# A fp32 hybrid SSD block on one core: sums of the second merge branch taken inside the group norms, SiLU by three tiles, and first loads and splits of each stage issued sooner

## Chip, core and metric

The kernel runs on one core of a Trainium2 chip. The metric is the device time of one execution in microseconds (us). Every number below comes from the timed runs of the kernel, or from one profiled execution of it.

## What is computed

One block on `x` of 1024 rows by 1024 columns, all in float32: a norm, an input projection to 8 fields, a Mamba-2 scan (SSD) with a group norm, a short gated convolution, two gated branch projections and an output projection, then a SwiGLU with 2816 hidden columns and a last norm.

```python
u = h @ w_in                                   # h = rmsnorm(x, norm_mix_w)
z, xbc, dt_raw, s_b, s_c, s_x, g_a, g_b = jnp.split(u, IN_SPLITS, axis=-1)
xbc = silu(causal_depthwise_conv(xbc, ssd_conv_w) + ssd_conv_b)
y = ssd_chunked_scan(xs32, dt, a, bm32, cm32) + d_skip * xs32
y = y * silu(z)
yg = y.reshape(bsz, seqlen, SSD_GROUPS, SSD_INNER // SSD_GROUPS)          # 4 groups of 512
yg = yg * lax.rsqrt(jnp.mean(yg * yg, axis=-1, keepdims=True) + EPS)
branch_a = (yg * ssd_norm_w) @ w_ssd_proj
branch_b = (s_b * causal_depthwise_conv(s_c * s_x, sconv_w)) @ w_sconv_proj
h = x + (sigmoid(g_a) * branch_a + sigmoid(g_b) * branch_b) @ w_o
h = h + (silu(n @ w_gate) * (n @ w_up)) @ w_down                          # n = rmsnorm(h, norm_ffn_w)
return rmsnorm(h, final_norm_w)
```

## The kernel before

Every large product is one level of Winograd-Strassen: seven products (numbers n, in the order 1, 2, 6, 5, 7, 3, 4) of block sums such as `T1` to `T4` of the right operand and `S1` to `S4` of the left. Each fp32 operand is split into a high and a low part (names that end in h and l: `wh`/`wl` of a weight, `qh`/`ql` and `gh`/`gl` of a merge chunk, `th`/`tl` of rows), and a product is three matmuls, high by high, low by high, high by low. ACT (ScalarE) makes the high parts, DVE (VectorE) the low ones; a matmul on TensorE (PE) that needs a low part waits for DVE.

The stages follow each other, and the order of the work is written out by hand, so each engine executes its list in that order. All tiles of 4 KB per partition come from one pool of 47 pages; a load into a page waits until its last user is done. SP issues nearly all loads and stores, in one list.

1. Start, 0 to about 74 us: rows of `x` are normed (`rows_sq`, `rows_scale`), transposed on PE (tiles `pt`), split, and the first pairs of weights are multiplied. The second half of the rows (`second_half`) follows between these.
2. Slots of the input projection, to about 605 us.
3. Direct tiles, to about 994 us: 22 weight slabs `ws` (6 for `z`, 16 for the gates `ga`, `gb`), a plain product each (tile `pr`, matmuls at L81 to L83). Between them runs the SSD scan (loads `bc`, `x`, `ab`, `eb`; matmuls `pxt`, `poff`, `pdg`), and after each group and half of the rows its norm: `z` is loaded, POOL multiplies (L508), ACT squares, DVE reduces, the factor goes to DRAM and back as a broadcast tile (`rs_d`, `rbc`), DVE scales the rows (L538) and they are stored to `y_g`. `y_sums` then loads two groups back (`br<-y_g`), makes the sums `T1` to `T4` (L720 to L724) and stores them to `yt_d`.
4. Merge, to about 1290 us: chunks of three products (`gv` for branch b, `gy` for branch a, `go` for `w_o`); a chunk is 24 matmuls of 512 columns for a pair of k-tiles. `Stream.step` loads four chunks ahead and splits two ahead; `ms.ahead(loads, splits)` does the first of these while the last direct tiles run.
5. FFN units to about 1745 us, whose first rows (`h1_rows`, `fill`, `put`) are normed, transposed and split while the last chunks of `go` run, then the down product (`ds`) and the last norm.

Of the kernel before, what the change touches and what calls it, by code (L numbers as in the profile page):

```python
# [13 lines left out]
P = 128  # L14
# [4 lines left out]
G = 4  # L19
# [20 lines left out]
def hybrid_block(ctx: ExitStack, tc: tile.TileContext, x, nmw, w_in, cw, cb, dtb, alog, dsk, snw,  # L40
# [194 lines left out]
    nc.sync.dma_start(ra, cw[0].rearrange("k (i p) -> (k i) p", p=P))  # L235
    rb = cp.tile([80, P], F32, name="rb")
    nc.sync.dma_start(rb[0:8, :], nmw.rearrange("o (i p) -> (o i) p", p=P))
    nc.sync.dma_start(rb[8:16, :], nfw.rearrange("o (i p) -> (o i) p", p=P))
    nc.sync.dma_start(rb[16:40, :], cb.rearrange("o (i p) -> (o i) p", p=P))
    nc.sync.dma_start(rb[40:56, :], snw.rearrange("o (i p) -> (o i) p", p=P))  # L240
    nc.sync.dma_start(rb[56:80, :], scw[0].rearrange("k (i p) -> (k i) p", p=P))
# [5 lines left out]
    nc.sync.dma_start(d2, dsk.rearrange("o (i j) -> (o i) j", j=2))  # L247

    dtbc = cp.tile([H, 1], F32, name="dtbc")
    nc.sync.dma_start(dtbc, dtb.rearrange("o h -> h o"))  # L250
    al = cp.tile([P, 1], F32, name="al")
    for q in range(4):
        nc.sync.dma_start(al[32 * q:32 * q + 32, :], alog.rearrange("o h -> h o"))
# [94 lines left out]
    halves, norms = {}, []  # L348
# [147 lines left out]
    def norm(g, hf, y0, y1):  # L496
# [204 lines left out]
    def yk(l, k):  # L701

        return (k // 4) * 8 + 4 * l + k % 4
# [5 lines left out]
    def y_sums(q):  # L709

        store = None
        for r in range(4):
            r1, r2 = page("br", HB), page("br", HB)
            for t, g in ((r1, 2 * q), (r2, 2 * q + 1)):
                nc.sync.dma_start(t.rearrange("p a l -> p (a l)"), y_d[4 * g + r])
            if store is not None:
                store()
            yield
            t = page("bt", HB)
            V.tensor_add(t[:, 0, :], r1[:, 0, :], r1[:, 1, :])  # L720
            V.tensor_add(t[:, 1, :], t[:, 0, :], r2[:, 1, :])
            yield
            V.tensor_add(r1[:, 1, :], r1[:, 1, :], r2[:, 1, :])
            V.tensor_add(r2[:, 0, :], r2[:, 0, :], t[:, 1, :])  # L724
            yield

            def store(r=r, t=t, r1=r1, r2=r2):
                for f, o in (("T1", t[:, 0, :]), ("T2", t[:, 1, :]), ("T3", r1[:, 1, :]), ("T4", r2[:, 0, :])):
                    nc.sync.dma_start(yt_d[f][(4 * q + r) * P:(4 * q + r) * P + P, :], o)
        store()  # L730
        yield

    def all_weight_sums():
        yield from weight_sums("S", sc_d, [(wsc, a, wsc, 512 + a, a, 256) for a in (0, 256)])
        yield from weight_sums("S", ss_d, [(wssd, 1024 * q + a, wssd, 1024 * q + 512 + a, 512 * q + a, 256)
                                           for q in range(2) for a in (0, 256)])
# [231 lines left out]

    def z_raw(i):
        hold = []  # L970

        def f(ps, hf):
            if hf == 0:
                hold.append(page("gt"))
# [199 lines left out]
    def ffn_phase():  # L1174
# [182 lines left out]
        while ms.at < len(ms.chunks):  # L1357
# [4 lines left out]
            if c.n in (7, 4):  # L1362
                for _ in range(3):
                    next(rows, None)
# [96 lines left out]
        for i, (_, pe, ev) in enumerate(rest):  # L1461
            load_to(14 + i)
            while later and next(later[0], 0) == 0:
                later.pop(0)
            pe()
# [3 lines left out]
            if i >= len(rest) - 4:  # L1469
                ds.ahead(i - len(rest) + 5, i - len(rest) + 2)  # L1470
# [43 lines left out]
    for p in first:  # L1514
        p.x.load()
# [194 lines left out]
```

## Time and profile before

| | us |
|---|---|
| median of 3 timed runs | 1966.7 (1964.54 to 1967.37) |
| profiled execution, its own time | 1965.9 |
| span of the profiled execution | 1964.1 |
| outside the span | 1.8 |
| PE busy | 1903.3 of the span |
| DVE, ACT, POOL busy | 1294.5, 984.2, 176.4 |

A row of the timeline or of a group gives the start, the busy time, the engine, the line, the operation and the tiles (written tile, arrow, read tiles). A bracket at the end gives the idle time of that engine just before and what ended it. In a table of windows `PEclk` is the mean granted clock of TensorE, as a share of full speed (1.00 is 2.4 GHz, 0.50 is 1.2 GHz).

### The profile page before, as it was taken

How to read it: one execution, taken by the hardware profiler on the slowest of the kernel's cores; microseconds unless marked ns; L12 is line 12 of the kernel's file. 1: busy time of each engine (PE TensorE's matmuls, PEld its weight loads, DVE VectorE, ACT ScalarE, POOL GpSimd, SP SyncE). 2: the span in 40 equal slices, each digit the busy share in tenths (PEclk: the TensorE clock that was granted, in tenths of full speed). 3: DMA queues.
4: the chain of work that ended last, by engine and by line, in shares of the span. 5: the costliest groups of instructions: out<-in, count | busy, mean ns of one | idle time of the engine just before them, and what ended most of it. 6: DMA issues, size and time to landing. Idle time of an engine off the chain costs nothing.

```text
span 1964.1 us, 24428 instructions
## 1 busy us (share of the span) xinstructions
PE 1903.3 (97%) x8917; PEld 1560.3 (79%) x8917; DVE 1294.5 (66%) x1674; ACT 984.2 (50%) x1547; POOL 176.4 (9%) x156
## 2 busy tenths in 40 slices
PE   5999999999998999998999999989999999999998
PEld 4678888888886887887878888878888888878886
DVE  6757877777774779787868547867444444456465
ACT  5444444444446997866556454455333333335433
POOL 0001111111100011110200000101121112100000
PEclk9999999999999999998999999989999999999999
DMA  5087998899959567776889766834888888868552
GB/s 176 22 218 202 220 239 211 240 240 236 266 155 265 180 204 226 234 254 210 289 332 388 260 224 208 205 124 103 231 192 193 215 198 201 208 241 303 193 185 116
DMA packets 350833, 422.49 MB, mean 215 GB/s; under 512 B 19752, under 2 KB 226424, under 8 KB 350712
## 3 DMA queue, kind: packets, MB, share of 16 engines
q1 hardware_dynamic: 304248, 353.80, 54.7%
q0 software_dynamic: 43296, 55.58, 17.7%
q10 hardware_dynamic: 3168, 11.54, 1.5%
q8 instruction: 70, 1.15, 0.2%
q14 instruction: 51, 0.42, 0.1%
HBM read 328.95 MB, written 145.24 MB: 241 GB/s over the span
## 4 chain that ended last, share of the span: by engine, by line
PE 55%; DVE 3%; DMA 2%; ACT 2%; issue 1%; SPq 0%; ACTq 0%; DVEq 0%
PE gb L664 5%; PE gb L665 5%; PE gb L663 5%; PE fb L665 4%; PE fb L664 4%; PE fb L663 4%; PE gd L665 4%; PE gd L664 4%; PE gd L663 4%; PE fd L663 3%; PE fd L664 3%; PE fd L665 3%; PE pr L81 2%; PE pr L83 2%; PE pr L82 2%; PE pdg L483 1%
## 5 line engine op out<-in xcount | busy, mean ns | idle before, releaser
L77 DVE TENSOR_TENSOR wl<-ws,wh 128x1024 fp32r<-128x1024 f32 x77 | 94.0, 1222 | 123.2 <-ACT wh L76 123.2
L664 PE MATMUL gb<-ql,gh 128*128 128x512 f32 x432 | 169.6, 393 | 3.7 <-DVE ql L77 3.7
L663 PE MATMUL gb<-qh,gh 128*128 128x512 f32 x432 | 169.6, 393 | 3.1 <-ACT qh L76 3.1
L665 PE MATMUL gb<-qh,gl 128*128 128x512 f32 x432 | 168.9, 391 | 0.0
L83 PE MATMUL pr<-th,wl 128*128 128x512 f32 x352 | 139.0, 395 | 7.6 <-DVE wl L996 7.6
L81 PE MATMUL pr<-th,wh 128*128 128x512 f32 x352 | 145.5, 413 | 0.0
L663 PE MATMUL fb<-th,wh 128*128 128x512 f32 x352 | 138.5, 393 | 2.6 <-ACT th L76 2.0
L665 PE MATMUL fb<-th,wl 128*128 128x512 f32 x352 | 138.0, 392 | 0.8 <-DVE wl L77 0.8
L664 PE MATMUL fb<-tl,wh 128*128 128x512 f32 x352 | 138.2, 393 | 0.5 <-DVE tl L77 0.5
L82 PE MATMUL pr<-tl,wh 128*128 128x512 f32 x352 | 138.2, 393 | 0.0
L663 PE MATMUL gd<-qh,gh 128*128 128x512 f32 x324 | 126.0, 389 | 0.0
L664 PE MATMUL gd<-ql,gh 128*128 128x512 f32 x324 | 126.0, 389 | 0.0
L665 PE MATMUL gd<-qh,gl 128*128 128x512 f32 x324 | 126.0, 389 | 0.0
L76 ACT ACTIVATE qh<-cb 128x1024 fp32r<-128x1024 f32 x98 | 100.0, 1020 | 40.7 <-PE gb L664 17.2
L77 DVE TENSOR_TENSOR ql<-cb,qh 128x1024 fp32r<-128x1024 f32 x98 | 115.9, 1182 | 3.2 <-ACT qh L76 3.0
L665 PE MATMUL fd<-th,wl 128*128 128x512 f32 x264 | 102.7, 389 | 0.0
L663 PE MATMUL fd<-th,wh 128*128 128x512 f32 x264 | 102.7, 389 | 0.0
L664 PE MATMUL fd<-tl,wh 128*128 128x512 f32 x264 | 102.7, 389 | 0.0
L74 DVE SCALAR_TENSOR_TENSOR gl<-ca,gh 128x1024 fp32r<-128x1024 f32 (+1 forms) x60 | 70.6, 1177 | 43.4 <-ACT gh L73 43.4
L664 PEld LDWEIGHTS gb<-ql,gh 128*128 128x128 f32 x432 | 81.8, 189 | 21.2 <-DVE ql L77 4.3
L663 PEld LDWEIGHTS gb<-qh,gh 128*128 128x128 f32 x432 | 81.8, 189 | 20.8 <-ACT qh L76 3.8
L665 PEld LDWEIGHTS gb<-qh,gl 128*128 128x128 f32 x432 | 81.8, 189 | 17.0
(309 smaller groups left out, 4725.0 us busy)
## 6 DMA issues: line engine op xcount, KB each, us to landing
ws<-in_w_in_dram SPq DMA_DIRECT2D x80, 512.0 KB, 7.7
ws<-in_w_gate_dram SPq DMA_DIRECT2D x77, 256.0 KB, 3.8
ws<-in_w_up_dram SPq DMA_DIRECT2D x77, 256.0 KB, 4.1
ca<-u_d SPq DMA_DIRECT2D x35, 512.0 KB, 6.2
ab<-ac_d SPq DMA_DIRECT2D x32, 512.0 KB, 6.0
xbc_d<-cv SPq DMA_DIRECT2D x24, 512.0 KB, 3.2
ws<-ws POOLq DMA_DIRECT2D x22, 512.0 KB, 6.3
wd_d<-in_w_down_dram SPq DMA_DIRECT2D x20, 512.0 KB, 11.7
```

What stands on the lines that cost most here:

```text
L74: nc.vector.scalar_tensor_tensor(lo, src, -1.0, hi.bitcast(F32), op0=ALU.mult, op1=ALU.subtract)
L76: nc.scalar.activation(hi, src, AF.Copy)
L77: nc.vector.tensor_sub(lo, src, hi.bitcast(F32))
L81: nc.tensor.matmul(o, lh, rh, start=first, stop=False)
L82: nc.tensor.matmul(o, lh, rl, start=False, stop=False)
L83: nc.tensor.matmul(o, ll, rh, start=False, stop=last)
L483: nc.tensor.matmul(pdg[64 * i:64 * i + 64, r * P:(r + 1) * P], xx[:, 0, 2 * r + i, :], ab[:, 2 * r + i, :], start=True, stop=True)
L663: nc.tensor.matmul(o, lh, rh, start=first, stop=False, skip_group_check=True)
L664: nc.tensor.matmul(o, lh, rl, start=False, stop=False, skip_group_check=True)
L665: nc.tensor.matmul(o, ll, rh, start=False, stop=last, skip_group_check=True)
```

## The change

In the order of the program:

- Start. The small loads `ra` and `rb` are issued on ACT's queue, and `d2`, `dtbc`, `al` after the first weight slabs. One row tile of each half is scaled by POOL instead of ACT. On PE the first half's 32 transposes come first, with the first weight pairs and the first half of the step-size product right behind them; the second half's transposes follow after the first product of all three pairs.
- `pump_scan()` is called at `left == 8` instead of 4: the first loads of the scan come ahead of the store of a `z` tile and of the first direct slab on SP.
- The six direct `z` tiles are evicted with `Copy`, and SiLU is applied to three tiles at a time, in place, before their stores.
- `y_sums` is gone. The norm keeps the pages of the first half of a group (`kept`), and after the second half it forms the four sums with DVE adds of 128x1024 and stores them. With that the k-halves of the branch are inside a group (`yk`, the regrouped sums of `wssd`), and rows of the second half that only fed the sums are no longer stored.
- `ms.ahead` is called before a direct tile instead of after it, and `ds.ahead` before the matmuls of an FFN step.
- The steps of the first FFN rows are given to the last four chunks of `go` as 2, 4, 6 and 2 instead of 3 each.

```diff
@@ start
-    nc.sync.dma_start(ra, cw[0].rearrange("k (i p) -> (k i) p", p=P))
+    nc.scalar.dma_start(ra, cw[0].rearrange("k (i p) -> (k i) p", p=P))
...
-    r0 = rows_scale(*a0, act=(2, 3))
+    r0 = rows_scale(*a0, act=(2,), pool=(3,))
...
+    for k in range(4):
+        turn_rows(r0, k)
+    turned_out(raw0, 0)
+    turned_out(raw0, 1)
+    p0.hi("A1")
+    turned_out(raw0, 2)
+    turned_out(raw0, 3)
+    p0.lo("A1")
+    for k in range(4, 8):
+        turn_rows(r0, k)
+    every(put("B11", raw0[0]))
+    p0.pe(1)
+    wdt_split()
+    steps_pe(0, 0)
...
+    r1 = rows_scale(*a1, act=(2,), pool=(3,))
...
@@ norm of a group
-            nc.sync.dma_start(y_d[4 * g + r][:, o], z)
+            if hf == 0 or r > 1:
+                nc.sync.dma_start(y_d[4 * g + r][:, o], z)
             if r % 2:
                 yield
-        if g % 2 and hf:
-            aux.append(y_sums(g // 2))
+        if hf == 0:
+            kept[g] = ys
+            return
+
+        b11, b21 = kept.pop(g)
+        b12, b22 = ys
+        t1, t2 = page("s1", HB), page("s2", HB)
+        for t, a, b, f in ((t1, b11, b12, "T1"), (t2, t1, b22, "T2"), (b12, b12, b22, "T3"), (b21, b21, t2, "T4")):
+            V.tensor_add(t, a, b)
+            nc.sync.dma_start(yt_d[f][256 * g:256 * g + 256, :].rearrange("(k p) f -> p k f", p=P), t)
+            yield
...
@@ z tiles
-            nc.scalar.activation(hold[0][:, hf * 512:hf * 512 + 512], ps, AF.Silu)
-            if hf:
-                nc.scalar.dma_start(z_d[i], hold.pop())
+            nc.scalar.activation(z_held[-1][1][:, hf * 512:hf * 512 + 512], ps, AF.Copy)
+            if hf and len(z_held) == 3:
+                for k, t in z_held:
+                    nc.scalar.activation(t, t, AF.Silu)
+                    nc.scalar.dma_start(z_d[k], t)
+                z_held.clear()
...
@@ FFN
-            if c.n in (7, 4):
-                for _ in range(3):
-                    next(rows, None)
+            for _ in range({(7, 0): 2, (7, 2): 4, (4, 0): 6, (4, 2): 2}.get((c.n, c.k), 0)):
+                next(rows, None)
...
+            if i >= len(rest) - 4:
+                ds.ahead(i - len(rest) + 5, i - len(rest) + 2)
             pe()
             ev()
             if i + 2 < len(rest):
                 rest[i + 2][0]()
-            if i >= len(rest) - 4:
-                ds.ahead(i - len(rest) + 5, i - len(rest) + 2)
...
@@ end of the slots, direct tiles
-        if left == 4:
+        if left == 8:
             pump_scan()
...
     for i in range(len(direct)):
+        ms.ahead(i - len(direct) + 4, i - len(direct) + 2)
         direct_tile(i)
-        ms.ahead(i - len(direct) + 4, i - len(direct) + 2)
```

First place, SP's list around 590 us, at the end of the slots. Before (`z_d` is the store of a `z` tile, `ws` a slab of a direct tile; the others are loads of the scan):

```order
L597 DMA z_d_151<-u_4272 128x1024
L597 DMA z_d_152<-u_4333 128x1024
L165 DMA ws_4417<-in_w_in_dram 128x8x128
L359 DMA bc_4454<-xbc_d_137 128x256
...
L363 DMA x_562_4459<-xbc_d_123 128x512
L363 DMA x_562_4459<-xbc_d_124 128x512
L373 DMA ab_4462<-ac_d 128x1024
L373 DMA ab_4464<-ac_d 128x1024
L381 DMA eb_4466<-e_d 64x4x128 x2
L165 DMA ws_4499<-in_w_in_dram 128x8x128
```

The same place of the change:

```order
L609 DMA z_d_145<-u_4272 128x1024
L361 DMA bc_4376<-xbc_d_131 128x256
...
L365 DMA x_552_4381<-xbc_d_117 128x512
L365 DMA x_552_4381<-xbc_d_118 128x512
L375 DMA ab_4384<-ac_d 128x1024
L375 DMA ab_4386<-ac_d 128x1024
L383 DMA eb_4388<-e_d 64x4x128 x2
L609 DMA z_d_146<-u_4333 128x1024
L165 DMA ws_4432<-in_w_in_dram 128x8x128
L165 DMA ws_4499<-in_w_in_dram 128x8x128
```

The ten loads of the scan moved ahead of the second store of a `z` tile and of the first direct slab, which now is eleven rows further down.

Second place, DVE's list where the direct tiles end and the merge begins (about 994 us). L538 (L540 in the change) scales rows of the last group's norm with `rbc`; `gl` and `ql` are the low parts of a merge chunk, the first pair those of chunk 0. Before:

```order
L538 SCALAR_TENSOR_TENSOR y_7657<-y_7657,cols,rbc_8318 128x512 x2
L74 SCALAR_TENSOR_TENSOR gl_8365<-ca_8184,gh_8364 128x1024
L77 TENSOR_TENSOR ql_8369<-cb_8186,qh_8368 128x1024
L538 SCALAR_TENSOR_TENSOR y_7658<-y_7658,cols,rbc_8318 128x512 x2
L74 SCALAR_TENSOR_TENSOR gl_8386<-ca_8289,gh_8385 128x1024
L77 TENSOR_TENSOR ql_8390<-cb_8291,qh_8389 128x1024
```

The same place of the change (L553 are the adds that make the four sums):

```order
L74 SCALAR_TENSOR_TENSOR gl_8278<-ca_8032,gh_8277 128x1024
L77 TENSOR_TENSOR ql_8282<-cb_8034,qh_8281 128x1024
L540 SCALAR_TENSOR_TENSOR y_7657<-y_7657,cols,rbc_8309 128x512 x2
L540 SCALAR_TENSOR_TENSOR y_7658<-y_7658,cols,rbc_8309 128x512 x2
L553 TENSOR_TENSOR s_1254_8352<-y_7196,y_7657 128x1024
L553 TENSOR_TENSOR s_1255_8353<-s_1254_8352,y_7658 128x1024
L553 TENSOR_TENSOR y_7657<-y_7657,y_7658 128x1024
L553 TENSOR_TENSOR y_7197<-y_7197,s_1255_8353 128x1024
L74 SCALAR_TENSOR_TENSOR gl_8372<-ca_8169,gh_8371 128x1024
L77 TENSOR_TENSOR ql_8376<-cb_8171,qh_8375 128x1024
```

The pair of chunk 0 moved ahead of the rows that wait for `rbc`; the pair of chunk 1 now stands behind all four of these and four adds of 128x1024.

## Rows read from the trace of the kernel before

**Rows 1.** Top of the page of the whole run: the span, and busy time of each engine with its share of the span and its instructions.

```profile
span 1964.1 us, 24428 instructions
PE 1903.3 (97%) x8917; PEld 1560.3 (79%) x8917; DVE 1294.5 (66%) x1674; ACT 984.2 (50%) x1547; POOL 176.4 (9%) x156
```

**Rows 2.** Who kept PE waiting over the whole run: engine, tile and line that waited, what it waited for, us in total, times, longest us.

```profile
PE pc L1521 <- DMA ra<-in_ssd_conv_w_dram: 9.6, 1, 9.6
PE pr L83 <- DVE wl L996: 7.6, 2, 6.8
PE pxt L420 <- DMA bc<-xbc_d: 4.0, 1, 4.0
PE gb L664 <- DVE ql L77: 3.7, 2, 2.8
PE pt L148 <- DVE hn L137: 3.3, 2, 3.0
PE poff L469 <- ACT st L476: 3.2, 1, 3.2
PE gb L663 <- ACT qh L76: 3.1, 1, 3.1
PE fb L663 <- ACT th L76: 2.0, 1, 2.0
```

**Rows 3.** Windows around these waits: start and end, length, busy time of PE, PEld, DVE, ACT, POOL with the number of instructions, granted clock of PE, busy share of the DMA engines, GB/s.

```profile
13.00:28.00 15.00, 9.98 (x45) 7.89 (x45) 11.27 (x21) 10.46 (x16) 0.00 (x0) 1.00 1.07 342
28.00:36.00 8.00, 5.46 (x16) 3.57 (x16) 6.25 (x10) 6.82 (x10) 0.00 (x0) 0.57 0.13 44
604.00:609.00 5.00, 1.04 (x5) 0.54 (x3) 0.00 (x0) 0.94 (x1) 0.70 (x1) 1.00 1.11 295
904.00:916.00 12.00, 5.20 (x33) 3.85 (x33) 9.48 (x15) 6.38 (x17) 0.00 (x0) 0.88 0.98 345
916.00:924.00 8.00, 8.00 (x29) 7.01 (x28) 7.09 (x14) 3.89 (x13) 0.00 (x0) 0.55 0.79 239
1288.00:1297.00 9.00, 5.59 (x19) 3.84 (x19) 5.46 (x12) 5.61 (x7) 0.00 (x0) 0.81 0.00 0
1312.00:1325.00 13.00, 10.49 (x35) 7.89 (x34) 9.83 (x17) 7.21 (x13) 0.00 (x0) 0.74 0.30 123
```

**Rows 4.** Timeline of DVE at the start (row scaling) and, with POOL's only elementwise work in the trace, around 760 us: start, us, engine, line, operation, tiles, count.

```profile
12.36 1.42 DVE L137 TENSOR_SCALAR xn<-x,nr 128x1024 f32<-128x1024 f32 x2
...
758.68 5.46 POOL L508 TENSOR_TENSOR y<-y,z 128x1024 f32<-128x1024 f32 x2 [41.40 <-PE pst L83]
759.00 2.89 DVE L444 TENSOR_TENSOR xw<-xx,xw 128x512 fp32r<-128x512 f32 x1
764.61 0.68 DVE L470 TENSOR_TENSOR xx<-poff,eb 128x512 f32<-128x512 f32 x1
```

**Rows 5.** Timeline of SP, ACT and PE where the scan and the direct tiles begin, with one row of what SP waited for between 590 and 625 us.

```profile
587.85 4.03 SPq L597 DMA_DIRECT2D z_d<-u  x2
591.92 0.65 SPq L165 DMA_DIRECT2D ws<-in_w_in_dram  x1
592.67 9.15 SPq L359 DMA_DIRECT2D bc<-xbc_d  x4
601.93 1.16 SPq L363 DMA_DIRECT2D x<-xbc_d  x2
...
SPq L359 <- PE pd L664: 5.4, 1, 5.4
...
608.06 1.06 ACT L993 ACTIVATE wh<-ws 128x1024 fp32r<-128x1024 f32 x1 [6.50 <-DMA ws<-in_w_in_dram]
616.46 0.40 PE L81 MATMUL pr<-th,wh 128*128 128x512 f32 x1
```

**Rows 6.** Timeline of DVE where `y_sums` runs ahead of the low part of a direct slab, and of PE, which waits for that part.

```profile
903.71 0.69 DVE L720 TENSOR_TENSOR bt<-br 128x512 f32<-128x512 f32 x1 [5.72 <-DMA br<-y_g]
...
909.18 1.22 DVE L442 TENSOR_TENSOR ab<-ab,cbm 128x1024 f32<-128x1024 f32 x1
...
915.38 0.79 PE L83 MATMUL pr<-th,wl 128*128 128x512 f32 x1 [6.80 <-DVE wl L996]
```

**Rows 7.** Timeline of DVE and PE where the merge begins.

```profile
994.27 1.42 DVE L538 SCALAR_TENSOR_TENSOR y<-y,cols,rbc 128x512 f32<-128x512 f32 x2 [9.93 <-DMA rbc<-rs_d]
...
997.09 0.50 PE L663 MATMUL gb<-qh,gh 128*128 128x512 f32 x1 [3.09 <-ACT qh L76]
998.54 0.79 PE L664 MATMUL gb<-ql,gh 128*128 128x512 f32 x1 [0.95 <-DVE ql L77]
...
1003.35 0.40 PE L663 MATMUL gb<-qh,gh 128*128 128x512 f32 x1
1003.58 0.39 PE L664 MATMUL gb<-ql,gh 128*128 128x512 f32 x1
```

**Rows 8.** Timeline of PE, DVE and ACT at the first FFN rows, and of PE at the first chunk of the down product.

```profile
1290.51 1.42 DVE L137 TENSOR_SCALAR hn<-h,nr 128x1024 f32<-128x1024 f32 x2
...
1291.41 0.30 PE L148 MATMUL pt<-ident,hn 128*128 128x128 f32 x1 [2.97 <-DVE hn L137]
1314.76 3.88 ACT L76 ACTIVATE th<-br 128x1024 fp32r<-128x1024 f32 x4
...
1747.20 0.50 PE L664 MATMUL gb<-ql,gh 128*128 128x512 f32 x1 [2.75 <-DVE ql L77]
```

More of the change, by code (lines that the diff above doesn't have):

```diff
@@ L345, in time_steps @@
         side.append(rest())
-    halves, norms = {}, []
+    halves, norms, kept = {}, [], {}
     def want(i, part):
@@ L701, in yk @@
     def yk(l, k):
-        return (k // 4) * 8 + 4 * l + k % 4
+        return k // 2 * 4 + 2 * l + k % 2
     def v_sums(k):
         return weight_sums("T", vt_d, [(v_g[0], k * P, v_g[1], k * P, k * P, 256)])
[L709 to L731, printed above, removed]
     def all_weight_sums():
         yield from weight_sums("S", sc_d, [(wsc, a, wsc, 512 + a, a, 256) for a in (0, 256)])
-        yield from weight_sums("S", ss_d, [(wssd, 1024 * q + a, wssd, 1024 * q + 512 + a, 512 * q + a, 256)
-                                           for q in range(2) for a in (0, 256)])
+        yield from weight_sums("S", ss_d, [(wssd, 512 * g, wssd, 512 * g + 256, 256 * g, 256) for g in range(G)])
         yield from weight_sums("T", wo_d, [(wo, a, wo, 512 + a, a, 256) for a in (0, 256)])
@@ L966, in slot @@
         p.ev(n)
+    z_held = []
     def z_raw(i):
[L970 removed]
         def f(ps, hf):
             if hf == 0:
[L974 to L977 removed]
+                z_held.append((i, page("gt")))
+            nc.scalar.activation(z_held[-1][1][:, hf * 512:hf * 512 + 512], ps, AF.Copy)
[4 more added lines that the diff above has]
+                z_held.clear()
         return f
@@ L1515, in hybrid_block, with wdt_split, steps_pe @@
         p.x.load()
+    small_loads()
     loaded[0] = NF
+    steps_ps, wdt_hl = [], []
+    def wdt_split():
+        for d in range(2):
+            t = sp.tile([P, 512], F32R, tag="st", name=nm("wdt"))
+            wdt_hl.append(t[:, 0:KT * H].rearrange("p (k h) -> p k h", h=H))
+        nc.scalar.activation(wdt_hl[0], wdt_s, AF.Copy)
+        V.tensor_sub(wdt_hl[1], wdt_s, wdt_hl[0].bitcast(F32))
+    def steps_pe(hf, part):
+        wh, wl = wdt_hl
+        if part == 0:
+            steps_ps.append(bank("ts"))
+        names = ((("B11",), ("B21",)), (("B11", "T1"), ("B22",)))[hf][part]
+        todo = [(n, k) for n in names for k in range(4)]
+        for j, (n, k) in enumerate(todo):
+            bh, bl = half_b(n, k)
+            kw = 4 * part + k
+            mmc(steps_ps[hf][:H], wh[:, kw, :], wl[:, kw, :], bh, bl, j == 0 and part == 0,
+                j == len(todo) - 1 and part == 1)
     a0 = rows_sq(xt[0:4], "x", "avav")
@@ L1557, in second_half @@
                 raw1[k // 4].append(page("br", HB))
-            pt = bank("pt")
-            for i in range(4):
-                nc.tensor.transpose(pt[:, i * P:(i + 1) * P], r1[i][:, k * P:(k + 1) * P], ident)
+            turn_rows(r1, k)
+            pt = turned.pop(k)
             o = k % 4 // 2, k % 2
@@ L1565, in second_half @@
                                    op0=ALU.mult, op1=ALU.subtract)
-            yield
-        raw0[0].clear()
-        for k in range(2):
-            nc.sync.dma_start(b12_d[k], raw1[0][k])
-        every(put("T1", t1))
-        yield
+            if k == 3:
+                raw0[0].clear()
+                for j in range(2):
+                    nc.sync.dma_start(b12_d[j], raw1[0][j])
+                every(put("T1", t1))
+            yield
         every(put("T2", t2))
@@ L1586, in second_half @@
         yield
[L1588 to L1608 removed]
     gen = second_half()
[L1610 removed]
+    turns = {3: 2, 4: 2, 5: 2, 6: 2, 7: 1, 9: 1, 11: 1, 14: 1}
     for i in range(7 * NF):
[L1612 removed]
+        if i >= NF:
+            slot(i)
         make(i)
```

86 lines of the change are left out of this document (40 added, 46 removed).

## Prediction

> **What bounds the kernel.** I read the top of the page first: PE is busy 1903.3 of 1964.1 us, 97% [rows 1]. The matmuls of the change are the same in number and shape, so all that can be won is PE's idle time, 61 us, and the time in which PE runs at half clock. The list of who kept PE waiting says where the idle time is [rows 2], and the reader is to see that it is not spread out: a few single waits of 2 to 7 us, each at the border of a stage or where one DVE list is late. [...] So each part of the change is priced by the stall that it touches plus the half clock behind it, and everything that it does to ACT, POOL or DMA away from those places costs nothing: PE hides it.
>
> **Start.** The first matmuls on `ra` cannot begin before 9.6 us, and the rows' norm follows the loads of `x`; the change leaves that. What it can win lies in 13 to 36 us. There PE idles 5.0 us in the first window and 2.5 in the second, and the clock of 0.57 takes 0.43 x 8 = 3.4 more: 10.9 us [rows 3]. With 32 transposes first and three pairs and half of the step product behind them PE has work from about 17 us on. What comes back is one wait for the second half's rows, which are normed later: by the rows' durations (norm, 1.42 for two rows on DVE, then POOL's row [rows 4]) they are ready about 35 us, where PE arrives at 33: 2.3 us, and about 2 at half clock. POOL's `tensor_scalar` is not in the trace. It lies between a DVE row, 0.71, and POOL's multiply of the same 128x1024 with two inputs, 5.46/2 = 2.73 [rows 4]; I take 2, being nearer to POOL's own row. Sum 10.9 - 4.3 = 6.6; I take 6 and keep 1 to 9.5: DVE is busy 11.3 of 15 us there [rows 3], so it can become the limit.
>
> POOL's multiply stretched a DVE instruction of 128x512 beside it from 0.68 to 2.89 [rows 4]. The Trainium skill, SBUF — State Buffer, section SBUF: two separate sides, says that DVE and GpSimd share one port pair under an exclusive lock, and that the loser blocks for a whole instruction; it speaks against giving rows to POOL, and the rows of 760 us agree with it. By that rule the two new POOL rows would hold DVE up by their whole length, and the start would gain 1 rather than 6.
>
> **End of the slots.** Before, SP issues the slab of the first direct tile at 591.92 and then the scan's loads, whose first `bc` waits 5.4 us for a page and which arrive late: PE waits 4.05 for them [rows 2, 5]. In the change the ten loads go first. Their issues take 9.15 - 5.4 = 3.75 for four and 1.16 for two [rows 5], some 2.4 for four more at 0.6 each: 7.3. The slab thus is issued about 4.5 us later (the second store of `z` before it had waited itself), and 2.25 MB more stand ahead of it, 7.6 us at the 295 GB/s of that stretch [rows 3]. It landed at 608.06, and the first direct product ran at 616.46, 8.4 later, since ACT makes its high part first and the rows' parts behind it [rows 5]. I take 6 us later, between 4.5 and 7.6. What is behind that product is 6 later; against that the later wait of 3.25 for `st` [rows 2], on an ACT that has one table load less to do there, goes away. The 4.05 wait goes too, but the wait for the slab stands in its place. Net a loss of 3, with 3 gained if the slab is not later at all, and 6 lost if it is 9 later.
>
> **SiLU of `z` in threes.** ACT loses some fifteen table loads and gains six passes of 128x1024. ACT ends no PE wait in the direct tiles except the one just counted, so this is 0, hidden by PE.
>
> **Sums in the norm.** Before, DVE stands 5.72 us in `y_sums` for rows that it loads back, and the low part of a slab comes late behind it [rows 6]: PE waits 6.8, and the clock behind it costs 0.45 x 8 = 3.6, in all 10.4 [rows 2, 3]. The change has nothing to load there. It puts 16 adds of 128x1024 at 1.22 (L442 is one [rows 6]) for 32 of 128x512 at 0.69: 19.5 us of DVE for 22.1. Without the 5.72 and the two adds of the loaded rows (1.4) the low part for which PE waits until 915.38 [rows 6] is there about 908.3; PE comes to it at 915.38 - 6.80 = 908.6. That is little to spare, so I take 10 gained, 8 to 10.4.
>
> **Start of the merge.** PE waits 3.1 for `qh` and 0.95 for `ql` [rows 2, 7], because the splits of chunk 0 stand behind rows that wait for `rbc` until 994.27. In the change they stand ahead, and chunk 0 starts at once, at 994.0. But the wait moves on: chunk 1's low parts now stand behind four rows (2 x 1.42) and four adds (4 x 1.14, back to back), that is 994.3 + 2.8 + 4.6 + 2.3 for the pair = 1004, and chunk 0's 24 matmuls, 0.23 apart [rows 7], are done at 999.5. PE waits 4.3 in place of 4.05, with the same half clock behind it, and SP's next chunk loads stand behind the stores of these adds. I take 1 lost, 2 gained to 3 lost.
>
> **First FFN rows.** PE waits 3.3 for `hn` and 2.0 for `th` [rows 2], and the clock takes 0.19 x 9 = 1.7 and 0.26 x 13 = 3.4 [rows 3]: 10.4. In the change the first transposes stand one chunk (5.5 us) later, when `hn`, whose two DVE rows end at 1291.9 [rows 8], has long been done; and `th`, of which ACT made four in 3.88 us at the last moment [rows 8], is made for the first two a chunk earlier. New is a wait for a PSUM bank, since the evictions of one chunk stand behind the splits of the next: 0.5. I take 8 gained, 5 to 10.4.
>
> **Down product.** PE waits 2.75 for `ql` [rows 8]. Its split moves ahead of the last FFN step's matmuls; the tiles of `ds` were loaded steps earlier, and the eviction it now precedes has a chunk of time: 2.5 gained, 1.5 to 2.7.
>
> **Sum.** -6 + 3 + 0 - 10 + 1 - 8 - 2.5 = -22.5. The profiled execution took 1965.9, 0.8 below the median of 1966.7, so 1965.9 - 22.5 = 1943.4; I say 1943.5.
>
> **Rivals.**
>
> 1. *POOL or DVE limits the start* (the lock above, or the squares and splits that crowd DVE): the start gains 1. 1948.5. The stretched instruction at 760 us speaks for it, DVE's two rows being issued first against it. 0.16.
> 2. *The slab is not late*: the DMA engines drain the scan's loads while the second `z` store is still waiting. Then the transition gains 3 instead of losing 3, and the start reaches its 9: 1934.5. 0.13.
> 3. *The late work stays late elsewhere*: the adds hold a slab's low part as the loaded sums did, so 908's stall stays (10 not gained): 1953.5. 0.08.
> 4. *Slower:* the four adds of each group's norm hold up the next slab at all four places, each time a stall like 908's with its half clock, 10.4. Then 4 x 10.4 = 41.6 more: 1985. It is slower than before by more than can be told once each of the four costs over (22.5 + 3.9)/4 = 6.6 us. For it speaks that a single late DVE list did cost that much, against it that DVE does less in sum and waits for no load. 0.03.
> 5. *The removed waits are replaced one by one*: the stage borders are bound by what they load, the FFN rows gain nothing, the slab comes 9 late: 1943.4 + 8 + 3 + 10 = 1964, no change that can be told. 0.03.
>
> The forecast itself holds 0.57, with a range of its own of 1938 to 1949.
>
> **Range and chances.** About 0.2%, 3.9 us, is what a measurement of this kernel can tell from no change. Rivals 4 and 5 give the chance of no change, 0.03, and of slower, 0.03; all other cases are faster, 0.94. The range runs from rival 2 to a little past rival 3: 1933 to 1956, which leaves out rivals 4 and 5 and little else.
>
> **What would show it.** PE's list of waits without the 6.8 on `wl`, without the 3.3 on `hn` and the 2.0 on `th`, and without the 2.75 before the down product; in place of the 4.05 on `bc` a longer wait for a slab's `wh` or for `th` behind it near 610 us; and in place of the wait for `qh` at the merge one for the low parts of chunk 1, four to five us, about 1000 us. At the start a wait of 2 to 3 for rows that POOL scaled. The granted clock below 1.00 in one or two windows fewer. The prediction is wrong if the slab of the first direct tile lands more than 9 us later, if the loss at the merge runs on into chunks 2 and 3 because their loads come late, or if waits for low parts appear behind the adds in the scan.

## The result and the profile after

The changed kernel takes 1950.6 us (median of 4 runs, 1947.6 to 1951.4) against 1966.2 for the kernel before in the same job (4 runs, 1964.5 to 1967.4): a ratio of 0.9918, 95% interval 0.9901 to 0.9935, so 15.6 us or 0.8% faster. The forecast was 1943.5 with a range of 1933 to 1956. The sign and the order of size are right; 7 us of the gain are missing: some 4 at the start and 8.6 in a stall that the prediction did not have, less 6 that came out better than forecast at the later borders.

The profiled execution took 1949.9 (1965.9 before). Top of its page: span, and busy time of each engine with its share of the span and its instructions.

```profile
span 1948.2 us, 24338 instructions
PE 1891.2 (97%) x8917; PEld 1553.1 (80%) x8917; DVE 1291.0 (66%) x1658; ACT 965.8 (50%) x1536; POOL 179.5 (9%) x158
```

PE has the same 8917 matmuls as in [rows 1] and is busy 12.1 us less with them: that is half clock that is gone. Its idle time went from 60.8 to 57.0. So the idle time has hardly shrunk; it has moved, as the list of who kept PE waiting shows (engine, tile and line that waited, what for, us in total, times, longest).

```profile
PE pt L1543 <- DVE xn L137: 8.8, 4, 6.1
PE pq L523 <- DVE sa L518: 7.7, 2, 6.7
PE pr L81 <- ACT wh L983: 7.0, 1, 7.0
PE pr L83 <- DVE wl L986: 7.0, 3, 6.0
PE pc L1533 <- DMA ra<-in_ssd_conv_w_dram: 4.5, 1, 4.5
PE gb L676 <- DVE ql L77: 3.1, 1, 3.1
```

Against [rows 2]: the waits for `bc`, `st`, `hn`, `qh` and the FFN's `th` are gone from its head. The wait of 6.0 for `wl` is not the one of 6.8 before: it ends at 621.7 us, behind the 7.0 for `wh`, where the direct tiles begin. New is one of 6.7 for `sa`, the squares of a group's norm. The 6.1 for rows of `xn` stands ahead of the very first transposes, in place of most of the 9.6 for `ra`: PE begins these at 14.35 us, where before it began them at 13.17. The wait for the second half's rows, which the change moved back, is the small one that ends at 38.43:

```profile
14.35 0.48 PE L1543 MATMUL pt<-ident,xn 128*128 128x128 f32 x1 [6.12 <-DVE xn L137]
...
38.43 1.71 PE L1543 MATMUL pt<-ident,xn 128*128 128x128 f32 x7 [1.14 <-DVE xn L137]
```

Windows of after (start and end, length, busy time of PE, PEld, DVE, ACT, POOL with instructions, granted clock, DMA share, GB/s), three of the stretches of [rows 3] and five others:

```profile
28.00:36.00 8.00, 8.00 (x36) 6.29 (x35) 4.97 (x11) 2.70 (x4) 0.00 (x0) 1.00 0.00 0
36.00:44.00 8.00, 6.36 (x27) 4.97 (x26) 7.52 (x12) 3.42 (x5) 1.62 (x1) 0.79 0.07 26
612.00:624.00 12.00, 3.56 (x8) 2.37 (x9) 5.38 (x6) 8.77 (x16) 0.00 (x0) 0.50 0.76 204
916.00:924.00 8.00, 8.00 (x55) 6.59 (x54) 3.59 (x11) 6.92 (x16) 0.00 (x0) 1.00 0.51 150
968.00:976.00 8.00, 4.55 (x21) 3.43 (x19) 0.21 (x1) 2.60 (x3) 2.85 (x2) 1.00 0.61 227
976.00:984.00 8.00, 4.79 (x15) 4.19 (x16) 5.88 (x13) 2.32 (x4) 0.00 (x0) 0.57 0.57 164
994.00:1010.00 16.00, 12.86 (x57) 10.34 (x56) 12.49 (x13) 6.97 (x9) 0.00 (x0) 1.00 0.96 353
1312.00:1325.00 13.00, 13.00 (x76) 11.30 (x75) 11.33 (x19) 9.07 (x12) 0.00 (x0) 1.00 0.01 1
```

The same windows of before at the places where after stalls:

```profile
612.00:624.00 12.00, 12.00 (x49) 9.70 (x48) 6.98 (x10) 11.91 (x28) 0.00 (x0) 0.83 0.83 244
968.00:976.00 8.00, 8.00 (x38) 6.52 (x37) 5.24 (x11) 3.46 (x6) 5.14 (x2) 1.00 0.87 336
976.00:984.00 8.00, 7.70 (x39) 6.25 (x38) 5.81 (x12) 1.84 (x4) 0.00 (x0) 1.00 0.72 267
```

The reader is to see three stretches healed (28 to 36, 916 to 924 and 1312 to 1325 run at full clock with PE busy throughout) and two that are newly ill: 612 to 624, with PE busy 3.6 of 12 us at half clock, where before it was busy throughout, and 968 to 984, a stall with half clock behind it where before there was none.

How far PE has got is read by comparing the start of the same matmul, found by its count within its tile, in both traces. The differences, after less before, in us:

```
place in the program             stands at   this step   forecast
start (88 us)                       -1.9        -1.9       -6
slots, to 590 us                    -1.1        +0.8        0
end of slots, first direct tile     +1.1        +2.2       +3
direct tiles, to 890 us             +1.8        +0.7        0
sums in the norm (to 974 us)        -9.0       -10.8      -10
new stall at a group's norm         -0.4        +8.6        -
start of the merge (1032 us)        -3.0        -2.6       +1
first FFN rows (1356 us)           -13.1       -10.1       -8
down product (1760 us), to the end -16.0        -2.9       -2.5
```

The steps add up to -16.0, the difference of the two profiled executions, where -22.5 was forecast. They vary from one execution to the next, most of all early in the program: in a second profiled execution of the changed kernel the start is -0.9 in place of -1.9, the new stall +9.6 in place of +8.6 and the merge -1.9 in place of -2.6, while the FFN rows and the down product are the same to 0.1. So an edit is read at its own place below, and not by the time of a single run.

### The profile page after: what moved, and what is told of

Read it like the earlier page. It is cut to its first block, busy times and chain, and to the rows that moved or that the text cites. A ratio compares the mean times of both kernels' runs of the same rounds, so it can differ in the third digit from the quotient of the medians.

```text
span 1948.2 us, 24338 instructions
## 1 busy us (share of the span) xinstructions
PE 1891.2 (97%) x8917; PEld 1553.1 (80%) x8917; DVE 1291.0 (66%) x1658; ACT 965.8 (50%) x1536; POOL 179.5 (9%) x158
## 4 chain that ended last, share of the span: by engine, by line
PE 49%; DVE 3%; DMA 2%; ACT 1%; issue 1%; SPq 0%; ACTq 0%; DVEq 0%
PE gb L676 5%; PE gb L675 5%; PE gb L677 5%; PE fb L677 4%; PE fb L676 4%; PE fb L675 4%; PE gd L676 4%; PE gd L677 4%; PE gd L675 4%; PE fd L677 3%; PE fd L676 3%; PE fd L675 3%; PE pr L81 1%; PE pr L83 1%; PE pr L82 1%
```

## The experiments

Each changes the kernel of the change, but for one that starts from the kernel before. Single runs are compared with the changed kernel's profiled execution (1949.9), timed ones by ratios to the kernel before in the same job.

**The order of the merge and of the FFN rows alone.** The old order is put back at the merge, the first FFN rows and the down product.

```
-        ms.ahead(i - len(direct) + 4, i - len(direct) + 2)
         direct_tile(i)
+        ms.ahead(i - len(direct) + 4, i - len(direct) + 2)
...
-            for _ in range({(7, 0): 2, (7, 2): 4, (4, 0): 6, (4, 2): 2}.get((c.n, c.k), 0)):
-                next(rows, None)
+            if c.n in (7, 4):
+                for _ in range(3):
+                    next(rows, None)
...     (and ds.ahead moved back behind the evictions)
```

> The change with three of its late parts undone: the merge's and the down product's first loads and splits again after a direct tile and after an FFN step, and the first FFN rows again three steps to each of the four last chunks. The three places lie far apart, so one trace prices each. Between the change and before, PE's work came 2.6 to 3 us earlier behind the merge's start, 10 behind the first FFN rows and 2.9 behind the start of the down product. Theory that each border's wait is set by its own order alone: PE waits again about 3 us on the high part qh at the merge's start, 3 on hn and 2 on th at the FFN rows with a clock near 0.55 behind, and 2.75 on ql at the down product; span 12 to 16 us longer than the change's 1948.2, so 1960 to 1964. Rival, that part of these gains comes from the removed loads and stores of the sums (less on the DMA queues): the span grows by 8 or less.

1970.2, 20 above the changed kernel, and above the 12 to 16 that were expected. From its list of PE's waits:

```profile
PE gb L676 <- DVE ql L77: 4.8, 3, 2.8
...
PE pt L148 <- DVE hn L137: 3.2, 2, 3.0
PE gb L675 <- ACT qh L76: 3.1, 1, 3.1
...
PE fb L675 <- ACT th L76: 2.0, 1, 2.0
```

The four waits of [rows 2] come back at their old sizes. By the same matmul the merge costs 4.0, the FFN rows 9.8 and the down product 4.5, 18.4 in all (1.8 more was there before the merge, which this edit does not touch). The excess over the change's own gains has its rows too: at the down product the wait is the 2.8 of before, but the clock falls behind it (0.91 and 0.87 from 1744 to 1760), where in the kernel before it had stayed at 1.00. So the new order by itself is worth the whole gain at these places; what feeds them did not take over as the bound.

**The sums alone.** Put into the kernel before: the adds go into the norm, `y_sums` goes away, nothing is moved. This kernel leaves out the new pattern of signs in the column weights of the norm, so its values are wrong; the work is the same.

```
...     (rows of the second half that only feed the sums not stored; k halves inside a group)
-        if g % 2 and hf:
-            aux.append(y_sums(g // 2))
+        if hf == 0:
+            kept[g] = ys
+            return
+        b11, b21 = kept.pop(g)
+        b12, b22 = ys
+        t1, t2 = page("s1", HB), page("s2", HB)
+        for t, a, b, f in ((t1, b11, b12, "T1"), (t2, t1, b22, "T2"), (b12, b12, b22, "T3"), (b21, b21, t2, "T4")):
+            V.tensor_add(t, a, b)
+            nc.sync.dma_start(yt_d[f]..., t)
+            yield
...     (y_sums taken out)
```

> The kernel before with the sums alone: formed in the norm from kept pages, k halves inside the groups, nothing else of the change. Theory: the wait of 6.8 on wl at 908 goes with its half clock (10 us), and the wait on sa near 972 comes instead (8 to 9 us), so it is 0 to 3 us faster than before, 1963 to 1966. Rival: the wait on sa depends on the chunk loads that the change moved ahead of the last tiles on SP; then the sums alone bring 9 to 11 us: 1955 to 1957.

1966.3 (1964.2 to 1969.9, 10 runs), ratio 1.000, 0.9991 to 1.0009. From its list of PE's waits:

```profile
PE pq L521 <- DVE sa L516: 7.5, 2, 7.0
...
PE pr L83 <- DVE wl L981: 2.4, 5, 0.8
```

The wait of 6.8 for `wl` is gone (0.8 is now the longest of its kind), and a wait of 7.0 for `sa` stands in its place: by the same matmul a gain of 10.8 and a loss of 10.1. So the new stall belongs to the sums, not to any of the moves, and this part of the change by itself is worth nothing.

**What the sums hold up.** In the changed kernel the row sums' reciprocal roots `rst` go to HBM (`rs_d`) and come back spread over the partitions (`rbc`), and DVE's rows of the norm wait for that. Rows of the timeline of the changed kernel around it, of ACT, SP, DVE and PE (start, us, engine, line, operation, tiles; in brackets the idle time ahead and what ended it):

```profile
962.73 3.68 SPq L1107 DMA_DIRECT2D cb<-v_g  x2
963.05 0.27 ACT L530 ACTIVATE rst<-prt 4x128 f32<-4x128 f32 x1 [0.87 <-PE prt L528]
969.54 0.37 SPq L554 DMA_DIRECT2D yt_d<-y  x1
970.00 0.32 SPq L532 DMA_DIRECT2D rs_d<-rst  x1
975.79 1.41 DVE L540 SCALAR_TENSOR_TENSOR y<-y,cols,rbc 128x512 f32<-128x512 f32 x2 [10.26 <-DMA rbc<-rs_d]
979.21 1.84 PE L523 MATMUL pq<-ones,sa 128*128 128x1 f32 x8 [6.66 <-DVE sa L518]
```

In the list of what SP waited for between 955 and 975 us this store of the sums (L554) stands with

```profile
SPq L554 <- DMA gb_d<-gt: 3.1, 1, 3.1
```

and the kernel before has the same two steps, one line of SP and one of DVE, as

```profile
972.34 0.27 SPq L530 DMA_DIRECT2D rs_d<-rst  x1
...
978.43 1.41 DVE L538 SCALAR_TENSOR_TENSOR y<-y,cols,rbc 128x512 f32<-128x512 f32 x2 [1.78 <-DMA rbc<-rs_d]
```

In the changed kernel `rst` is ready at 963.3, but its store is issued at 970.0. Ahead of it in SP's list stand two loads of a merge chunk (`cb`), issued late (until 966.4) since the sums' stores ahead of them had waited for DVE, and then the last store of the sums, which waits 3.1 us for a transfer of `gt`, though it shares no data with it. DVE's rows start 12.7 us after `rst`, and the sum of the squares (`sa`), which is queued behind them on DVE, comes 6.66 late for PE. Before, `rst` started at 972.05, its store left at 972.34, and the rows started 6.4 us after it: the difference of 6.3 is about the 6.7 that the store stands in SP's list. The test is to move the sums' stores to another queue:

```
-            nc.sync.dma_start(yt_d[f]..., t)
+            nc.gpsimd.dma_start(yt_d[f]..., t)
```

> The change with the stores of the four sums of each norm issued on POOL's queue instead of SP's, so that on SP the store and the load of the next norm's factors (rs_d, rbc) stand behind none of them. In the change PE waits 6.66 us at 979 for sa, DVE's list stands 10.26 on rbc ahead of it, and rs_d was issued at 970.0, 6.7 us after its tile was ready at 963.3, behind a store that itself waited for an older DMA. Theory (SP's order): rs_d goes out at once, PE's wait for sa is gone with the half clock behind it, and the time is 7 to 9 us less than the change's: 1942 to 1944 by the median. Rival (DVE's list is simply longer by the adds): the wait for sa stays over 4 us, time within 2 us of the change.

1946.5 (1946.2 to 1948.6), ratio 0.9899, 0.9883 to 0.9916: 4 us below the changed kernel's median. PE's waits, and then the window of the merge:

```profile
PE gb L676 <- DVE ql L77: 4.5, 1, 4.5
...
PE pq L523 <- DVE sa L518: 2.7, 2, 1.6
```

```profile
994.00:1010.00 16.00, 11.54 (x40) 9.24 (x40) 10.88 (x10) 7.32 (x10) 2.17 (x3) 0.79 1.00 370
```

The stall falls from 6.7 to 1.6, and the merge begins 5.2 us sooner: that the stores in SP's queue made it is shown. But the gain is less than the 7 to 9 expected. PE now reaches chunk 1 of the merge earlier, waits 4.5 instead of 3.1 there, and the clock falls to 0.79 in that window where it had stayed at 1.00. By the same matmul the first stall gave up 7.3 us and the next one took 3.8 of them.

**The end of the slots: what comes first.** Two kernels change only the order of the loads there. One begins the scan four slots later (as late as needed for the slab to be issued ahead of it):

```
-        if left == 8:
+        if left == 4:
             pump_scan()
```

> The change with the scan's first loads issued again where they were (left == 4). Between the change and before PE came 2.2 us later behind this place. Theory that the place of these loads alone does it: PE's waits of 7.0 on wh and 6.0 on wl near 614 and 621 us are gone, those of about 4 on bc and 3 on st are back, and the span is 2 to 3 us shorter than the change's 1948.2: 1945 to 1946. Rival, that the wait of 3.25 on st was taken away by the SiLU in threes and stays away: the gain is 5 to 6, span 1942 to 1943.

The other leaves the scan's place and issues the slab ahead of it:

```
-        if left == 6:
-            direct[0][0].load()
         if left == 8:
+            direct[0][0].load()
             pump_scan()
```

> The change with the first direct slab loaded at the same place as the scan's first loads (left == 8) but ahead of them on SP. Undoing the move of the scan's loads gave 5.5 us at this place. Theory that only the order of the two on SP matters: the slab arrives at about 600 to 605 us, PE's waits of 7.0 and 6.0 for its parts are gone and bc's wait of 4 does not come back: 6 to 10 us less span than the change's 1948.2, 1938 to 1942. Rival: the slab waits for a page until PE has used it, and holds the scan's loads up behind it, so that PE waits for bc again: span 1942 to 1945.

1944.5 and 1944.5: single runs, each 5.4 to 5.5 below the changed kernel. Of the first, PE's waits; behind them, of the second, a row of SP and PE's waits.

```profile
PE pxt L422 <- DMA bc<-xbc_d: 3.9, 1, 3.9
...
PE pr L83 <- DVE wl L986: 2.1, 3, 0.9
```

```profile
583.87 11.42 SPq L361 DMA_DIRECT2D bc<-xbc_d  x4
```

```profile
PE pr L83 <- DVE wl L986: 5.0, 1, 5.0
...
PE pxt L422 <- DMA bc<-xbc_d: 2.5, 2, 1.5
```

In the first the two waits of 7.0 and 6.0 are gone and the wait for `bc` of [rows 2] is back at its old size (3.9); the wait of 3.2 for `st` stays away. In the second the four loads of `bc` take 11.4 us to issue (4.2 of it a wait for a matmul of PE, that is for a page), and a wait of 5.0 for `wl` stays.

That the two times are equal is chance. By the same matmul, from 590 to 660 us, the first gains 6.0 on the kernel before and the second 0.9, where the changed kernel loses 2.2. The second stood 3.0 us further ahead than the first when it came to 590 us, in a stretch that neither edit touches. So the step that the change took in the wrong order costs 8.2 us at its place, of which 5.4 were left at the end of this run, and having the slab first while keeping the scan early wins back only 3.1. The scan's earlier loads bought one wait of 4 us and cost 13 us of waits at half clock. That `st`'s wait, with the half clock behind it, stays away without them points to the SiLU in threes, the part of the change that is left there; no run has the SiLU alone.

**The start: POOL's rows and the order of the loads.** One kernel gives POOL's two rows to ACT:

```
-    r0 = rows_scale(*a0, act=(2,), pool=(3,))
+    r0 = rows_scale(*a0, act=(2, 3))
...     (the same for a1)
```

> The change with the third and fourth row of each half scaled by ACT again, none by POOL. In the change DVE's two rows took 2.29 us instead of 1.42 while POOL's row of 1.65 ran beside them, in both halves, and the start brought 1.9 us by the time of the matmuls at 88 us instead of the 6 forecast. Theory of the shared port: the two DVE rows are back at 1.42, PE's first transposes come about 0.9 us earlier, and the matmuls at 88 us stand 1.5 to 3 us earlier than in the change. Rival, that the start is limited elsewhere (the late row tile of x, the list of DVE): under 0.7 us at 88 us, since ACT's two rows in a row end as late as POOL's one.

Another issues the column weights on SP's queue, behind the rows of `x`:

```
-    nc.scalar.dma_start(ra, ...)
+    nc.sync.dma_start(ra, ...)
...     (the same for the five parts of rb)
```

> The change with ra and rb loaded on SP's queue again, behind the first four row tiles, as before; all else as in the change. In the change the load of the fourth row tile waited 3.6 us on SP for that of the second, since the loads on ACT's queue had taken the semaphores between, and the last square of the first half ended at 11.9 us where it ended at 10.6 before. Theory: it ends at 10.6 again, the first transposes start at about 13.1 instead of 14.35, and the matmuls at 88 us stand 1 to 1.5 us earlier. Rival, that ra then arrives late and holds the chain up as before (PE waits 9 us for it, and DVE copies its columns ahead of the norm's factors): under 0.5 us at 88 us.

1949.5 and 1948.8, single runs, too near 1949.9 to be read by their time. Rows of DVE, of the changed kernel, of the one without POOL's rows and of the one with the weights on SP:

```profile
10.70 1.23 DVE L115 SCALAR_TENSOR_TENSOR xn<-x 128x1024 f32<-128x1024 f32 x1 [3.73 <-DMA x<-in_x_dram]
13.54 2.29 DVE L137 TENSOR_SCALAR xn<-x,nr 128x1024 f32<-128x1024 f32 x2
13.61 1.67 POOL L133 TENSOR_SCALAR xn<-x,nr 128x1024 f32<-128x1024 f32 x1 [11.79 <-DVE nr L107]
```

```profile
11.73 1.23 DVE L115 SCALAR_TENSOR_TENSOR xn<-x 128x1024 f32<-128x1024 f32 x1 [4.90 <-DMA x<-in_x_dram]
14.58 1.42 DVE L137 TENSOR_SCALAR xn<-x,nr 128x1024 f32<-128x1024 f32 x2
```

```profile
0.74 1.81 SPq L231 DMA_DIRECT2D x<-in_x_dram  x4
8.45 1.23 DVE L115 SCALAR_TENSOR_TENSOR xn<-x 128x1024 f32<-128x1024 f32 x1 [1.86 <-DMA x<-in_x_dram]
```

Without POOL's row DVE's two rows take 1.42 again, as in [rows 4], instead of 2.29. The last row of `x` came 1.0 later in that run, so the two are compared from the last square on: from there to the matmul at 86 us it is 74.2 us without POOL's rows and 75.8 with them (75.3 to 75.9 in seven other runs that have them, and 74.2 again in the two below that do not). POOL's rows cost 1.1 to 1.7 us more than ACT's. In the changed kernel SP's four loads of `x` take 5.32 us to issue, of which 3.6 are a wait for an earlier one of them to land; meanwhile ACT issues `ra` and `rb` from 0.95 to 4.5 us. With these behind the rows of `x` on SP the four take 1.81, nothing waits, and the last square begins 2.3 us sooner. It is the loads on ACT's queue that held up SP's: the four take 5.1 to 5.3 us in all eight runs that have them there, and 1.8 in the five that do not. How much that is worth is less sure. At 86 us this run is 2.6 ahead of the changed kernel, but seven runs with the same start vary by 2.6 there themselves; it lies 1.0 ahead of the best of them.

**All of it together.** The scan at `left == 4`, the sums' stores on POOL's queue, and the splits of the merge one chunk further ahead:

```
-        ms.ahead(i - len(direct) + 4, i - len(direct) + 2)
+        ms.ahead(i - len(direct) + 4, i - len(direct) + 3)
```

> The change with three edits: the scan's first loads where they were (left == 4), the stores of the sums on POOL's queue, and the merge's splits one chunk further ahead of the last direct tiles, so that the low parts of chunk 1 stand ahead of the last norm's rows and adds on DVE. Priced apart: 5.5 us for the first; for the second 6.7 of wait with its half clock less 1.6 that stays, of which the wait at chunk 1 (4.5 with its half clock) took most back; the third takes that away, 4.5 and some 2 of clock. If these add, the time is 5.5 + 1.5 + 6 = 13 us less than the change's median of 1950.6: 1936 to 1940. If the wait at chunk 1 only moves on to chunk 2 or 3 (their loads stand behind y stores), 1942 to 1945.

1935.9 (1933.3 to 1937.6), ratio 0.9845, 0.9816 to 0.9873. The wait for `ql` is gone. The merge begins at 980.3 in this run, chunk 1 at 985.7, and the window there shows PE busy 10.00 of 10 us at full clock:

```profile
984.00:994.00 10.00, 10.00 (x46) 8.29 (x45) 6.77 (x7) 2.50 (x4) 2.61 (x4) 1.00 1.00 315
```

With both edits of the start as well:

> The three edits of c_three and two more at the start: ra and rb on SP's queue, and no row scaled by POOL. Measured apart, the first lets the last row tile of x arrive about 1.3 to 2.3 us sooner, and the second gives DVE's two rows back 0.87 us in each half; counted from the arrival of that row tile, the matmuls at 86 us came 75.3 to 75.8 us later with POOL's rows and 74.2 without. If both hold, 2.5 to 4 us less than c_three's median of 1935.9: 1932 to 1933.5. If the start is limited by the arrival of the rows alone, 1934 to 1935.

1932.9 (1930.9 to 1934.4), ratio 0.9832, 0.9817 to 0.9847: 33 us below the kernel before. The changed kernel, run again on the same chip, took 1950.4 (1947.3 to 1953.5) against 1965.7, ratio 0.9922, 0.9905 to 0.9938, with the same waits of 6 to 7 us for `wh`, `wl` and `sa` in its list.

> The change itself once more, on the same chip as c_five and c_six, to set them against it: 1950 us within 2.5 as in its first runs, with PE's waits of 6 to 7 us for wh, wl and sa at the same places. If those waits were an accident of one execution they would differ by more than 1.5 us here.

The scan's place alone had given 5.5 and the stores 4; with the splits a chunk further ahead it is 14 to 15 in all, since what the stores win is no longer given back at the merge: by the same matmul the merge is 6.1 ahead of the kernel before there, where with the stores alone it was 1.1 behind (the splits alone were not tried). The two edits of the start add 3, which the intervals don't tell from nothing. Two of the best kernel's waits of over 3 us in all stand at the start (9.8 for `ra`, 3.5 for `xn`); the others are

```profile
PE pq L523 <- DVE sa L518: 5.2, 2, 4.1
PE pxt L422 <- DMA bc<-xbc_d: 4.5, 2, 3.9
```

The wait for `sa` is 4.1 again, though no store of the sums stands in SP's list. Rows of POOL and DVE there:

```profile
957.74 5.20 POOL L510 TENSOR_TENSOR y<-y,z 128x1024 f32<-128x1024 f32 x2
958.52 4.96 DVE L540 SCALAR_TENSOR_TENSOR y<-y,cols,rbc 128x512 f32<-128x512 f32 x2 [0.70 <-DMA rbc<-rs_d]
```

The last store of the sums now stands in POOL's list, where it waits for DVE until 956.99, and POOL's multiplies of the next norm stand behind it. They come to lie beside DVE's two rows, which take 4.96 us instead of 1.41; in the changed kernel the multiplies began at 966.09 and were over before these rows began at 975.79. So the stores' new queue has a price of its own: by the same matmul this place costs 7.0 in the best kernel and 5.0 in the one without the edits of the start, against 8.6 in the changed kernel and 1.3 with the stores alone moved. No run separates this further.

Last, the scan two slots earlier in it (`left == 6`), to see whether the wait for `bc` is one for time:

> As c_five, with the scan's first loads issued two slots earlier (left == 6), right behind the first direct slab on SP. In c_three PE waits 4.03 us for bc at 605; with the slab ahead of the loads on SP it is not held up by them. If SP's order is all, the wait for bc shrinks to under 2 us and no wait for a slab's part takes its place: 3 to 5 us less than c_five. If the loads wait for a page until PE releases it, as they did in the kernel before, the two are within 1.5 us.

1934.1 (1933.7 to 1935.8), ratio 0.9842: no difference from 1932.9 that can be told, and the wait is 4.5 still. SP issues the four loads of `bc` from 586.42 to 596.03 here and from 587.60 to 597.14 in the kernel with four slots: asking two slots sooner brings them 1.1 us sooner. In the latter 5.5 us of it are a wait for a matmul of PE, for a page; in the former the trace names no releaser, and that it is the page there too is argued, not shown.

## Why the prediction was right or wrong

**What bounds the kernel: right.** What moved were PE's waits and the half clock. The busy time of DVE, ACT and POOL changed by -3.5, -18.4 and +3.1 us, which PE's time does not follow.

**Start, forecast -6, measured -1.9: mis-sized.** The stretch that was priced came out near its price. From 13 to 36 us PE is busy 20.6 of 23 us at full clock, against 15.4 before. The second half's rows cost what was set aside for them: waits of 0.5 and 1.1 and a clock of 0.79 from 36 to 44, 3.3 us where 2.3 and 2 were forecast. By these windows the start had won 5.2 us at 44 us, where the sum had 6.6; at 88 us 1.9 are left. That loss after 44 us is a term that the sum did not have. PE's idle time shows 0.9 of it, the rest no row here explains, and the kernels with both edits of the start lose as much there.

Two causes of what is missing before 44 us are shown. "The change leaves that" was wrong of the loads of `x`: the small loads moved to ACT's queue held up SP's fourth load, so that the last square starts at 10.70 and the first transposes 1.2 us later than before. And POOL's row took 1.67, between the bounds of 0.71 and 2.73, but beside it DVE's pair took 2.29 instead of 1.42; the sum had only POOL's time and not what it does to DVE. With both undone the start is 4.8 ahead of the kernel before. Rival 1 named POOL's part, and its gain of 1 was nearer than 6, but not the loads. DVE lost 0.87 us to POOL's row, not its whole 1.67. The Trainium skill, SBUF — State Buffer, section SBUF: two separate sides, has the loser of the shared port blocked for a whole instruction of the other. The rows can be read that way: POOL's row is recorded from 0.07 us after DVE's pair began, so it may itself wait for DVE's first row (0.71 of its 1.67) and then hold up the second. What the prediction took from the page, a delay by the whole recorded length, was too much. No run here has POOL's row alone.

**End of the slots, forecast +3, measured +2.2: the right sum of two terms that were both too small.** The slab landed at 613.3, 5.3 later than before (6 taken, 4.5 to 7.6), though it was issued 11.5 later and not 4.5, since the scan's loads took 15.5 us to issue and not 7.3. (The 2.25 MB ahead of it are 2.36 million bytes, 8.0 us at the rate used and not 7.6; by itself that moves no term.) PE's waits are on `wh` and `wl`, as said, and `st`'s wait shrank from 3.2 to 0.7. But the kernel with the scan's loads in their old place shows what each part is worth here: the earlier loads cost 8.2, and the rest gained 6.0. The half clock behind PE's long waits for the slab, and that behind `st`'s wait, were in neither term. That the sum came out is luck.

**SiLU in threes, 0: too small, as far as the runs show.** The 6.0 just named are the wait for `st` and the half clock behind it, and the SiLU is the part of the change left there; the prediction counted 3.25 of them in the term before. No run has the SiLU alone.

**Sums, forecast -10, measured -10.8 and then +8.6: a step that was missing.** The stall on `wl` went as forecast. But the sum counted the new adds only against DVE's next low part. Their stores stand in SP's queue ahead of the small store that the next half's norm is waiting for, which left 6.7 us late; that queue was named for the merge's loads ("SP's next chunk loads stand behind the stores") and not looked through at 963. Rival 4 expected stalls behind the adds at four places and through DVE; one came, through SP.

**Merge, forecast +1, measured -2.6: a term mis-sized.** The wait for chunk 1's `ql` is there, but is 3.15 instead of 4.3 (4.5 by the prediction's own terms, 1004 less 999.5), since the pair is done by 1002.4, not 1004 (0.9 less than the waits of before); and the clock stays at 1.00, so the half clock that was priced in did not come (1.8: 0.89 over 16 us before). That last part is luck: in the second run of the changed kernel the wait was 2.33 and the clock fell to 0.78 for 8 us, 1.7 us worth, and it fell behind the same wait in all five other kernels that have it.

**First FFN rows -8, measured -10.1; down product -2.5, measured -2.9: right.** The waits are gone, as are the clock's dips. The wait for a PSUM bank came, as 1.1 (a matmul of `gb` at 1293.7 that waits for DVE's add of the chunk before, L1133) where 0.5 was set aside.

The time lies nearest to rival 1's 1948.5, but not for its reason: about 4 us were lost at the start and 8.6 at the new stall, and 6 came back at the merge, the FFN rows and the down product. That the total is only 7 off is in part that these cancel.

## What to carry to other kernels

When a change puts new stores on a queue, go through that queue at each place where something small and urgent is issued (here 2 KB of row sums, 6.7 us late), and not only at the stage that the change is about. A wait that is removed makes PE arrive earlier at the next border: the list of waits should be walked on until one is found with time to spare, since the two borders that were mended alone gave 4 and 5.5 us, and with a third 14 to 15. The same goes for the queue that a store is moved to: on POOL's list the sums' stores held up POOL's multiplies. And two single runs of the same time need not be worth the same: each is read at the place of its edit. Whether the clock falls behind a wait of 2 to 4 us is not told by its length, so its price has two ends (below).

## What the runs showed of the hardware

- **The clock behind waits of like length.** At one place, the wait for chunk 1's `ql` at the merge, it went either way. Windows of the changed kernel, where the wait is 3.15, and of the one with the scan at `left == 4`, where it is 2.23:

```profile
1000.00:1004.00 4.00, 1.56 (x7) 1.30 (x8) 4.00 (x5) 0.00 (x0) 0.00 (x0) 1.00 1.03 340
1004.00:1008.00 4.00, 4.00 (x19) 3.31 (x18) 1.48 (x2) 1.06 (x1) 0.00 (x0) 1.00 1.01 373
```

```profile
992.00:996.00 4.00, 1.77 (x8) 1.15 (x7) 4.00 (x4) 0.44 (x1) 0.00 (x0) 0.98 1.05 408
996.00:1000.00 4.00, 4.00 (x12) 3.14 (x11) 1.61 (x2) 0.00 (x0) 0.00 (x0) 0.59 0.99 272
```

  The longer wait left the clock alone, the shorter one was followed by 0.59 (1.6 us lost). With the slab first it was 1.95 and then 0.57; with the stores on POOL's queue 4.46 and then 0.62 and 0.52, 3.4 us lost in 8. At the down product a wait of 2.75 in the kernel before left the clock at 1.00, and the same wait in two other kernels was followed by 0.86 and 0.87. What decides between them no run here settles.
- **DVE beside POOL.** A pair of 128x1024 rows on DVE took 2.29 us beside one POOL row of 1.67, and 1.42 without it: it lost half of POOL's recorded time, not all of it. Beside two of POOL's multiplies (5.20 together) a pair of 128x512 rows took 4.96 instead of 1.41, a loss of 3.55.
- **Arrival of the first loads.** The last row of `x` is waited for until 9.5 to 11.7 us in the eight runs whose loads at the start are issued in the same way. What is gained at the start by less than 2 us needs the rows, not the times.
